# Group norm of a pair's outputs by two whole-tile sums, with its squares on ScalarE

## The chip, the cores and the metric

The kernel runs on one core of one Trainium2 chip. The metric is the device time of one execution, in microseconds. The engines are PE (matrix products), DVE (vector work), ACT (activations and copies), POOL and SP; SP and ACT also issue DMAs. Each engine works through a queue of its own, and semaphores join them.

## The reference

One layer of a decoder trunk, 512 positions of width 2048, in float32. Half of the width is an RWKV-7 group of 16 heads of 64 channels. Its recurrence gives for each position and head a vector `y` of 64 outputs, which is then normalized over the 64 channels of its head:

```python
def head_group_norm(y, w, b):
    B, T, H, N = y.shape
    mean = jnp.mean(y, axis=-1, keepdims=True)
    var = jnp.mean(jnp.square(y - mean), axis=-1, keepdims=True)
    yn = (y - mean) * lax.rsqrt(var + GN_EPS)
    return yn.reshape(B, T, H * N) * w.astype(jnp.float32) + b.astype(jnp.float32)
```

A bonus term is added, the sum is multiplied by a gate, joined with the pooled half, projected by `w_out` and added to the input; a gated embedding and an RMS norm follow.

## The kernel before

The input is normalized and transposed once into 16 tiles of channels by positions, each split in two parts, `hhi` and `hlo`; every large product is three matmuls on such parts (`mm3`, L164). The projections are computed in units of 128 output columns, 48 matmuls of 128x512 each. A generator (`stream`, L461) yields them one after another, and `pump(n)` (L492) takes about `n` matmuls from it.

The RWKV group goes in 8 pairs of heads, j = 0 to 7. `recur(j, ...)` (L753) runs the recurrence of a pair over 8 chunks of 64 positions. It is a chain of small matmuls, DVE and ACT steps, with `pump` calls between them, so that PE works on projections while the chain moves. DVE meanwhile solves the triangular systems of the next pair (`invert`, L650). At the end of chunks 3 and 7 ACT copies four heads-by-chunk blocks of `py` into `ysb` (L827), a tile of 128 positions by 4 x 2 x 64 channels: 8 groups of 64 channels in each partition.

Then comes the group norm that the change rewrites (L838 to L852). `y8` is `ysb` seen as 8 groups. Each group gets a `bn_stats` and a `bn_aggr` on DVE, for mean and variance; 64e-5 is added; `rsqrt` (L142) makes the reciprocal root of the 8 variances in eleven steps on 128x8 numbers, an estimate from the bits and three Newton rounds (L143 to L151); and each group is scaled by a `tensor_scalar` with its own mean and factor (L851). `finish` (L854) is put on a list.

Next, `gather(j + 1)` (L678) starts the following pair: `decay_and_rate` (L517; its DVE steps are L526, L533 and the scan L534), transposes of `v` and `bk`, `pump(H4)`, `norm_key` (L563, its DVE step L568), `pump(H5)`, and only then the pending `finish` of pair j: PE transposes `ysb` into `pyt` (L858), ACT scales it into `yo` (L860), DVE adds the bonus and multiplies by the gate (L861, L862), and ACT's queue stores it. Behind that, DVE transposes `x1` (L723) for the small products `pq`, `pmv` and `px`, and `scale_key` takes a reciprocal of 128x512 (L572) and a product (L573). `prepare(j + 1)` (L577) has the DVE steps L591 to L601. Weights come in chunks through four buffers; each is rounded on ACT (L132) and its rest taken on DVE (L133).

The framework places each engine's instructions itself, by readiness and priority, so that steps of different functions interleave in a queue. PE's matmuls of this stage are pinned to program order (`pin`, L154). `issue_after` holds a step behind another, and `high_priority` draws the recurrence's steps forward.

Of the kernel before, what the change touches and what calls it, by code (L numbers as in the profile page):

```python
# [9 lines left out]
F32 = mybir.dt.float32  # L10
F32R = mybir.dt.float32r
I32 = mybir.dt.int32
AF = mybir.ActivationFunctionType
ALU = mybir.AluOpType

P = 128
# [7 lines left out]
C = 64  # L24
# [10 lines left out]
def trunk_kernel(ctx: ExitStack, tc: tile.TileContext, x, p, norm_g, w_in, mu, w0, w_up, a0, a_up,  # L35
                 k_k, k_a, r_k, ln_w, ln_b, w_pool, pool_scale, w_out, w_ple, w_pg, b_pg, final_g, out):
    nc = tc.nc
# [104 lines left out]
    def rsqrt(y, v, t):  # L142
        nc.vector.tensor_scalar(y.bitcast(I32), v.bitcast(I32), -0.5, float(0x5F3759DF), ALU.mult, ALU.add)  # L143
        nc.vector.tensor_scalar(v, v, -0.5, None, ALU.mult)
        for _ in range(3):
            if v.shape[-1] * v.shape[1] == 1:
                nc.vector.scalar_tensor_tensor(t, y, v, y, ALU.mult, ALU.mult)
            else:
                nc.vector.tensor_tensor(t, y, v, ALU.mult)
                nc.vector.tensor_tensor(t, t, y, ALU.mult)  # L150
            nc.vector.scalar_tensor_tensor(y, t, 1.5, y, ALU.add, ALU.mult)  # L151
# [55 lines left out]
    for kind, nm, j in jobs:  # L207
# [7 lines left out]
        else:  # L215
            g, i = j // 4, j % 2
# [124 lines left out]
    rw = s2a.enter_context(tc.tile_pool(name="rw", bufs=1))  # L341
# [411 lines left out]
    def recur(j, work, between):  # L753
        d = st_.pop(j)
        pw, ar, mt, bv, uv, bkn, mv, x1 = (d[n_] for n_ in ("pw", "ar", "mt", "bv", "uv", "bkn", "mv", "x1"))
# [79 lines left out]
            pass  # L835


        st = rw.tile([P, 8, 6], F32, name=f"st{j}", tag="st")  # L838
        mvr = rw.tile([P, 8, 2], F32, name=f"mvr{j}", tag="mvr")
        y8 = ysb.rearrange("p q (h c) -> p (q h) c", h=2)  # L840
        for i in range(8):
            nc.vector.bn_stats(st[:, i, :], y8[:, i, :])
        for i in range(8):
            nc.vector.bn_aggr(mvr[:, i, :], st[:, i, :])
        rs8 = rw.tile([P, 8, 1], F32, name=f"rs8{j}", tag="rs8")
        ve8 = rw.tile([P, 8, 1], F32, name=f"ve8{j}", tag="ve8")
        nc.vector.tensor_scalar(ve8, mvr[:, :, 1:2], 64e-5, None, ALU.add)
        nt8 = rw.tile([P, 8, 1], F32, name=f"nt8{j}", tag="nt8")
        rsqrt(rs8, ve8, nt8)
        for i in range(8):  # L850
            nc.vector.tensor_scalar(y8[:, i, :], y8[:, i, :], mvr[:, i, 0:1], rs8[:, i, :],  # L851
                                    ALU.subtract, ALU.mult)  # L852

        def finish():  # L854
            sg = need("g", j)
# [29 lines left out]
    for j in range(NJ):  # L885
        def between():
            pump(H3 if j + 1 < NJ else HC[2])
            if j + 1 < NJ:
                scores(j + 1)
                pump_to(H2)  # L890

        if j + 1 == NJ:
            pn.append(rw.tile([P, NT, DPLE], F32, name="pn", tag="ar", bufs=2))
            for h in range(2):
                nc.scalar.dma_start(out=pn[0][:, 2 * h:2 * h + 2, :],
                                    in_=p[256 * h:256 * h + 256, :].rearrange("(t p) q -> p t q", p=P))
        if j + 1 < NJ:
            prepare(j + 1)
        recur(j, invert(j + 1) if j + 1 < NJ else iter(()), between)
        if j + 1 < NJ:  # L900
            gather(j + 1)
# [276 lines left out]
```

## Time and profile before

| | |
|---|---|
| time, median of 3 runs | 1094.54 us (1093.39 to 1097.44) |
| time of the profiled execution | 1094.06 us |
| its span, first to last instruction | 1092.3 us |
| PE, DVE, ACT busy | 1067.4, 707.9, 448.2 us |
| mean granted clock of PE | 0.998 |

Rows of a timeline give start and length in microseconds, the engine, the line, the operation, the tile written and those read, and the shapes; in brackets stands the idle time ahead of the row and what ended it. "x4" merges four neighbours. A busy PE is not PE at its peak: matmuls of 128x512 overlap, so that each has a recorded length of about 0.39 us while they start about 0.23 us apart.

### The profile page before, as it was taken

To read this page: it belongs to the slowest core of one execution; us is meant where nothing else is said; L and a number is where in the kernel's file an instruction comes from. 1 tells how busy PE (TensorE), PEld (TensorE's weight loads), DVE (VectorE), ACT (ScalarE), POOL (GpSimd) and SP (SyncE) were. 2 spreads that over 40 slices of the span, in tenths; PEclk is the share of its full clock that TensorE was granted. 3 is DMA by queue.
4 is the path that set the end of the run, shared out by engine and by line. 5 is a ranking of instruction groups with operands and counts; after the bars stand their busy time and mean duration, and the time that the engine had idled before them with its cause. 6 is when DMAs were issued, how large, how long until landed. Compare 5 with 4: busy or idle time off the path is not lost.

```text
span 1092.3 us, 17194 instructions
## 1 busy us (share of the span) xinstructions
PE 1067.4 (98%) x6060; PEld 879.1 (80%) x6060; DVE 707.9 (65%) x1835; ACT 448.2 (41%) x917; POOL 74.4 (7%) x180
## 2 busy tenths in 40 slices
PE   5999999999999999999999999999999999999996
PEld 4888878888888888787888788888888888888885
DVE  6687867878779679678886956454433424445366
ACT  7633534435335335353443344544222222233337
POOL 2100010110110110100101101000000000000000
PEclk9999999999999999999999999999999999999999
DMA  7433433332423333333334242774534438454534
GB/s 233 116 97 97 112 92 79 102 101 72 127 81 102 105 91 89 95 83 90 94 93 120 79 138 94 231 242 163 171 123 141 164 97 261 129 187 147 174 105 154
DMA packets 178485, 138.56 MB, mean 127 GB/s; under 512 B 34677, under 2 KB 139742, under 8 KB 178398
## 3 DMA queue, kind: packets, MB, share of 16 engines
q1 hardware_dynamic: 157694, 103.89, 32.2%
q10 hardware_dynamic: 20704, 33.56, 9.5%
q8 instruction: 48, 0.79, 0.3%
q14 instruction: 39, 0.32, 0.1%
HBM read 118.02 MB, written 18.87 MB: 125 GB/s over the span
## 4 chain that ended last, share of the span: by engine, by line
PE 88%; DVE 5%; DMA 3%; ACT 2%; issue 1%; SPq 0%; ACTq 0%; DVEq 0%
PE acc_o L157 16%; PE acc_g L157 16%; PE zb L157 15%; PE zv L157 8%; PE zr L157 7%; PE zg L157 7%; PE zk L157 6%; DMA n<-nd 2%; PE py L157 2%; PE pple L157 2%; PE pu L157 2%; PE pm L157 1%; PE pp L157 1%; PE ps L157 1%; PE pmv L157 1%
## 5 line engine op out<-in xcount | busy, mean ns | idle before, releaser
L133 DVE TENSOR_TENSOR wlo_g<-raw_g,whi_g 128x512 fp32r<-128x512 f32 x84 | 56.9, 683 | 78.7 <-ACT whi_g L132 78.5
L157 PE MATMUL zb<-hhi,whi_b 128*128 128x512 f32 x256 | 106.3, 415 | 0.0
L133 DVE TENSOR_TENSOR wlo_o<-raw_o,whi_o 128x512 fp32r<-128x512 f32 x64 | 43.9, 690 | 92.3 <-ACT whi_o L132 92.2
L157 PE MATMUL zb<-hhi,wlo_b 128*128 128x512 f32 x256 | 100.5, 393 | 0.0
L157 PE MATMUL acc_o<-whi_o,ylo 128*128 128x512 f32 x256 | 100.2, 391 | 0.0
L157 PE MATMUL acc_o<-whi_o,yhi 128*128 128x512 f32 x256 | 99.9, 390 | 0.0
L157 PE MATMUL zb<-hlo,whi_b 128*128 128x512 f32 x256 | 99.8, 390 | 0.0
L157 PE MATMUL acc_o<-wlo_o,yhi 128*128 128x512 f32 x256 | 99.7, 389 | 0.0
L132 ACT CAST whi_g<-raw_g 128x512 fp32r<-128x512 f32 x84 | 51.9, 620 | 105.5 <-PE acc_g L157 60.3
L157 PE MATMUL acc_g<-whi_g,x2hi 128*128 128x512 f32 x208 | 81.2, 391 | 0.0
L157 PE MATMUL acc_g<-wlo_g,x2hi 128*128 128x512 f32 x208 | 81.0, 389 | 0.0
L157 PE MATMUL acc_g<-whi_g,x2lo 128*128 128x512 f32 x208 | 80.6, 389 | 0.0
L132 ACT CAST whi_o<-raw_o 128x512 fp32r<-128x512 f32 x64 | 39.9, 623 | 97.8 <-PE acc_o L157 97.8
L813 POOL TENSOR_SCALAR s0p<-sbd,pw 64x64 f32<-64x64 f32 x96 | 56.7, 590 | 338.5 <-DVE sbd L806 253.7
L132 ACT CAST whi_b<-raw_b 128x512 fp32r<-128x512 f32 x64 | 39.7, 620 | 87.1 <-PE zv L157 34.9
L133 DVE TENSOR_TENSOR wlo_b<-raw_b,whi_b 128x512 fp32r<-128x512 f32 x64 | 43.7, 684 | 34.2 <-ACT whi_b L132 33.0
L157 PEld LDWEIGHTS zb<-hhi,wlo_b 128*128 128x128 f32 x256 | 48.0, 188 | 11.0
L661 DVE TENSOR_TENSOR xw<-xw,tm 128x60 f32<-128x60 f32 (+24 forms) x248 | 51.9, 209 | 6.8
L157 PEld LDWEIGHTS acc_o<-wlo_o,yhi 128*128 128x128 f32 x256 | 48.1, 188 | 10.0
L157 PEld LDWEIGHTS acc_o<-whi_o,ylo 128*128 128x128 f32 x256 | 48.1, 188 | 9.9
L157 PEld LDWEIGHTS acc_o<-whi_o,yhi 128*128 128x128 f32 x256 | 48.1, 188 | 9.6
L157 PEld LDWEIGHTS zb<-hhi,whi_b 128*128 128x128 f32 x256 | 48.3, 189 | 8.4
(285 smaller groups left out, 2546.8 us busy)
## 6 DMA issues: line engine op xcount, KB each, us to landing
raw_b<-in_w_in_dram SPq DMA_DIRECT2D x64, 256.0 KB
raw_o<-in_w_out_dram SPq DMA_DIRECT2D x64, 256.0 KB
raw_g<-in_w_pg_dram SPq DMA_DIRECT2D x64, 256.0 KB
raw_k<-in_w_in_dram SPq DMA_DIRECT2D x32, 256.0 KB
raw_r<-in_w_in_dram SPq DMA_DIRECT2D x32, 256.0 KB
raw_v<-in_w_in_dram SPq DMA_DIRECT2D x32, 256.0 KB
raw_g<-in_w_in_dram SPq DMA_DIRECT2D x32, 256.0 KB
n<-nd SPq DMA_DIRECT2D x16, 256.0 KB
```

The costliest lines, as they stand in the source:

```text
L132: nc.scalar.copy(hi, raw)
L133: nc.vector.tensor_tensor(lo, raw, hi.bitcast(F32), ALU.subtract)
L157: i = nc.tensor.matmul(*a, **k)
L661: nc.vector.tensor_tensor(xw[:, 0:n_, s + 1:32], xw[:, 0:n_, s + 1:32], tm[:, 0:n_, 0:w_], ALU.add)
L813: nc.gpsimd.tensor_scalar(s0p[hc, :], nxt[hc, hc], pcn[hc], None, ALU.mult)
```

## The change

The statistics of the 8 groups are taken over the whole tile. A sum over the channels (L840) is multiplied by -1/64 (L841) and added to `y8` as a broadcast operand (L842); ACT squares the centred tile into `ysq`, which takes the place of the tile `mv` (L844); a second sum (L846), scaled and raised by 64e-5 (L848), goes to `rsqrt`; and one product with the broadcast factors (L851) scales the tile. The functions behind it are the same, and from here on their lines have numbers lower by one.

```diff
-        st = rw.tile([P, 8, 6], F32, name=f"st{j}", tag="st")
-        mvr = rw.tile([P, 8, 2], F32, name=f"mvr{j}", tag="mvr")
         y8 = ysb.rearrange("p q (h c) -> p (q h) c", h=2)
-        for i in range(8):
-            nc.vector.bn_stats(st[:, i, :], y8[:, i, :])
-        for i in range(8):
-            nc.vector.bn_aggr(mvr[:, i, :], st[:, i, :])
+        mn8 = rw.tile([P, 8, 1], F32, name=f"mn8{j}", tag="mn8")
+        nc.vector.tensor_reduce(mn8, y8, mybir.AxisListType.X, ALU.add)
+        nc.vector.tensor_scalar(mn8, mn8, -1.0 / C, None, ALU.mult)
+        nc.vector.tensor_tensor(y8, y8, mn8.to_broadcast([P, 8, C]), ALU.add)
+        ysq = rw.tile([P, 8, C], F32, name=f"ysq{j}", tag="mv")
+        nc.scalar.activation(ysq, y8, AF.Square)
+        ve8 = rw.tile([P, 8, 1], F32, name=f"ve8{j}", tag="ve8")
+        nc.vector.tensor_reduce(ve8, ysq, mybir.AxisListType.X, ALU.add)
         rs8 = rw.tile([P, 8, 1], F32, name=f"rs8{j}", tag="rs8")
-        ve8 = rw.tile([P, 8, 1], F32, name=f"ve8{j}", tag="ve8")
-        nc.vector.tensor_scalar(ve8, mvr[:, :, 1:2], 64e-5, None, ALU.add)
+        nc.vector.tensor_scalar(ve8, ve8, 1.0 / C, 64e-5, ALU.mult, ALU.add)
         nt8 = rw.tile([P, 8, 1], F32, name=f"nt8{j}", tag="nt8")
         rsqrt(rs8, ve8, nt8)
-        for i in range(8):
-            nc.vector.tensor_scalar(y8[:, i, :], y8[:, i, :], mvr[:, i, 0:1], rs8[:, i, :],
-                                    ALU.subtract, ALU.mult)
+        nc.vector.tensor_tensor(y8, y8, rs8.to_broadcast([P, 8, C]), ALU.mult)
```

The order of PE's matmuls is the same in both programs. On DVE and ACT it is not. A row below names the line, the operation, the tile written, the tiles read and the shape; the number behind a tile's name counts tiles. This is DVE in the kernel before, from the second Newton round of pair 0's `rsqrt` (`rs`, `nt`) to the reciprocal of the next pair's key norm (`kk`):

```order
L149 TENSOR_TENSOR nt_2347<-rs_2344,ve_2345 128x8
L526 TENSOR_TENSOR us_2598<-ur_2595,us_2598 64x128
L150 TENSOR_TENSOR nt_2347<-nt_2347,rs_2344 128x8
L151 SCALAR_TENSOR_TENSOR rs_2344<-nt_2347,rs_2344 128x8
L149 TENSOR_TENSOR nt_2347<-rs_2344,ve_2345 128x8
L533 TENSOR_SCALAR sig_2382<-sig_2382 128x512
L150 TENSOR_TENSOR nt_2347<-nt_2347,rs_2344 128x8
L534 SCALAR_TENSOR_TENSOR sig_2382<-seg,sig_2382 128x512
L151 SCALAR_TENSOR_TENSOR rs_2344<-nt_2347,rs_2344 128x8
L591 TENSOR_SCALAR kp_2605<-tha_2394,dprm 128x512
L851 TENSOR_SCALAR ysb_1663<-ysb_1663,mvr_2327,rs_2344 128x64 x5
```

In the changed program the same stretch of DVE ends with these rows, the last of them the product that completes pair 0's `ysb`:

```order
L723 STREAM_TRANSPOSE y_2489<-x_2258 32x256
L133 TENSOR_TENSOR wlo_b_3_1403<-raw_b_3_1400,whi_b_3_1402 128x512
L151 SCALAR_TENSOR_TENSOR rs_2334<-nt_2336,rs_2334 128x8
L370 SCALAR_TENSOR_TENSOR sv_2430<-zv_2227,prm,sv_2430 128x511
L149 TENSOR_TENSOR nt_2336<-rs_2334,ve_2332 128x8
L572 RECIPROCAL kk_2349<-kk_2349 128x512
L150 TENSOR_TENSOR nt_2336<-nt_2336,rs_2334 128x8
L596 TENSOR_TENSOR bk_2586<-kp_2587,ipw_2369 128x4x2x64
L151 SCALAR_TENSOR_TENSOR rs_2334<-nt_2336,rs_2334 128x8
L573 SCALAR_TENSOR_TENSOR kk_2349<-sk_2076,prm,kk_2349 128x512
L851 TENSOR_TENSOR ysb_1663<-ysb_1663,rs_2334 128x512
```

Before, the scalings of `ysb` stand ahead of L568, L723, L572 and all behind them. Now the transposes, the reciprocal and steps of `prepare` stand between the Newton steps, ahead of L851.

The second place is the beginning of the same work in pair 2, on DVE; `st` and `mvr` are the statistics, `us`, `sig`, `kp` and `ar` belong to pair 3. Before:

```order
L842 BN_STATS st_4253<-ysb_3576 128x6 x4
L844 BN_AGGR mvr_4254<-st_4253 128x2 x4
L847 TENSOR_SCALAR ve_4272<-mvr_4254 128x8
L143 TENSOR_SCALAR rs_4271<-ve_4272 128x8
L144 TENSOR_SCALAR ve_4272<-ve_4272 128x8
L149 TENSOR_TENSOR nt_4274<-rs_4271,ve_4272 128x8
```

And in the changed program:

```order
L840 TENSOR_REDUCE mn_4217<-ysb_3540 128x8
L841 TENSOR_SCALAR mn_4217<-mn_4217 128x8
L842 TENSOR_TENSOR ysb_3540<-ysb_3540,mn_4217 128x512
L526 TENSOR_TENSOR us_4492<-ur_4489,us_4492 64x128
L533 TENSOR_SCALAR sig_4255<-sig_4255 128x512
L534 SCALAR_TENSOR_TENSOR sig_4255<-seg,sig_4255 128x512
L846 TENSOR_REDUCE ve_4223<-ysq_4221 128x8
L591 TENSOR_SCALAR kp_4499<-tha_4267,dprm 128x512
L848 TENSOR_SCALAR ve_4223<-ve_4223 128x8
L594 TENSOR_TENSOR ar_4497<-sr_4040,pw_4259 128x4x2x64
```

Here the scan L534 of the next pair has moved ahead of the second sum. The four early statistics, which before ran in the loop behind chunk 3, are gone from there.

The third place is ACT behind the last copies of `py` into `ysb`, pair 0. Before:

```order
L827 COPY ysb_1663<-py_4_2023 64x256 x2
L524 CAST us_2598<-ur_2595 128x128
L532 ACTIVATE sig_2382<-pu_2379,dprm 128x512
L547 ACTIVATE tha_2394<-pa_2391,dprm 128x512
L690 COPY uv_2396<-pv_2397 64x4x128
```

And now:

```order
L827 COPY ysb_1663<-py_4_2023 64x256 x2
L844 ACTIVATE ysq_2330<-ysb_1663 128x512
L532 ACTIVATE sig_2364<-pu_2361,dprm 128x512
L547 ACTIVATE tha_2376<-pa_2373,dprm 128x512
L690 COPY uv_2378<-pv_2379 64x4x128
```

The Square stands ahead of the next pair's `sig`, and waits there for the subtraction; the cast L524 has moved behind the copies of `bkn`.

## The prediction

> **What bounds the kernel now.** I read the page first, then the list of waits of PE, then the timelines of PE, DVE and ACT around the first group norm, and last the windows at both ends of the span, for the clock.
>
> ```profile
> PE 1067.4 (98%) x6060; PEld 879.1 (80%) x6060; DVE 707.9 (65%) x1835; ACT 448.2 (41%) x917; POOL 74.4 (7%) x180
> ...
> PE py L157 <- DVE sbd L806: 1.9, 6, 0.6
> PE pu L157 <- ACT x L745: 1.0, 1, 1.0
> PE pu L157 <- DVE zs L784: 0.7, 2, 0.4
> ```
>
> PE is the bound: it is busy for 98% of the span, and behind the first 30 us it waits for only 1.9 + 1.0 + 0.7 = 3.6 us. DVE is free a third of the time. So work taken off DVE is worth almost nothing, and what DVE delivers late to PE costs its full length. PE's order is pinned; whatever it waits for holds every matmul behind it. The one delivery of the group norm to PE is `ysb`, which `finish` transposes into `pyt`. Here is DVE at the end of pair 0, and the transposes:
>
> ```profile
> 182.69 0.61 DVE L842 BATCH_NORM_STATS2 st<-ysb 128x6 f32<-128x64 f32 x4 [0.32 <-ACT ysb L827]
> 183.21 0.36 DVE L844 BATCH_NORM_AGGREGATE mvr<-st 128x2 f32<-128x6 f32 x4
> 183.61 0.17 DVE L847 TENSOR_SCALAR ve<-mvr 128x8 f32<-128x8 f32 x1
> 183.81 0.17 DVE L143 TENSOR_SCALAR rs<-ve 128x8 int32<-128x8 int32 x1
> ...
> 185.83 0.42 DVE L533 TENSOR_SCALAR sig<-sig 128x512 f32<-128x512 f32 x1
> 186.16 0.16 DVE L150 TENSOR_TENSOR nt<-nt,rs 128x8 f32<-128x8 f32 x1
> 186.28 1.22 DVE L534 TENSOR_TENSOR_SCAN sig<-seg,sig 128x512 f32<-128x512 f32 x1
> 187.43 0.14 DVE L151 SCALAR_TENSOR_TENSOR rs<-nt,rs 128x8 f32<-128x8 f32 x1
> 187.49 0.54 DVE L591 TENSOR_SCALAR kp<-tha,dprm 128x512 f32<-128x512 f32 x1
> 187.94 1.20 DVE L851 TENSOR_SCALAR ysb<-ysb,mvr,rs 128x64 f32<-128x64 f32 x5
> 189.06 0.68 DVE L133 TENSOR_TENSOR wlo_b<-raw_b,whi_b 128x512 fp32r<-128x512 f32 x1
> 189.66 0.75 DVE L851 TENSOR_SCALAR ysb<-ysb,mvr,rs 128x64 f32<-128x64 f32 x3
> 190.33 0.68 DVE L568 TENSOR_SCALAR kk<-pss 128x512 f32<-128x512 f32 x1
> 190.93 0.89 DVE L723 STREAM_TRANSPOSE y<-x 32x256 f32<-32x256 f32 x2
> 191.86 3.35 DVE L572 RECIPROCAL kk<-kk 128x512 f32<-128x512 f32 x1
> ...
> 191.43 0.60 PE L161 MATMUL pyt<-ident,ysb 128*128 128x128 f32 x4
> ```
>
> `ysb` is normalized at 189.66 + 0.75 = 190.41, and PE reaches `pyt` at 191.43: a margin of 1.0 us. From the first statistic (182.69) to PE's need there are 8.7 us. That deadline, not the length of the group norm, is what the change must meet.
>
> **The change part by part.** DVE works through its queue in order. Start to start, an operation of 512 elements holds it a little less than its recorded length, since neighbours overlap: 0.60 for 0.68 (189.06 to 189.66), 0.33 for L533, 1.15 for the scan, 0.45 for L591, 3.27 for the reciprocal's 3.35. A 128x8 step between two long ones costs 0.06 to 0.12; I take 0.08.
>
> *The arithmetic alone* gets shorter. Per pair, 8 statistics, 8 aggregations and 8 scalings (1.20 + 0.75 + 2 x 0.61 + 2 x 0.36 = 3.9 us) give way to two sums, an addition, a multiplication and a 128x8 step. No row shows a reduction of this size; its bounds are the one-input L533 (0.42) and the two-input L133 (0.68); I take 0.68, since L568, with one input too, takes as long. The broadcast operations have two inputs: 0.68. That is about 2.9 us. The Square on ACT is put between the two rows below, of 0.69 and 0.64, and a handoff to ACT costs 0.1 (`pw` starts at 187.60, the scan before it ends at 187.50): about 0.8 us in which this chain waits.
>
> ```profile
> 184.71 0.69 ACT L532 ACTIVATE sig<-pu,dprm 128x512 f32<-128x512 f32 x1
> ...
> 187.60 0.64 ACT L539 ACTIVATE pw<-sig 128x512 f32<-128x512 f32 x1 [0.57 <-DVE rs L151]
> ```
>
> *The order* is what changes most. A sum over the whole tile cannot start before the last `ysb` copy, so the four early statistics of the loop go, and the variance waits for ACT. Meanwhile `sig`, `tha` and `pw` of the next pair arrive, and the built program places one long operation of the next pair's preparation behind nearly every small step of `rsqrt`. In an in-order queue each is paid in full, the reciprocal among them. Pair 0: L840 starts at 182.69, the subtraction ends at 184.3, Square at 185.0, L846 starts at 185.1 and holds 0.60. Then come L533 0.33, scan 1.15, L591 0.45, L592 0.60, L593 0.33, two weight splits 1.20, L594 0.60, L568 0.60, the two transposes 0.80, L370 0.66, reciprocal 3.27, L596 0.60, L573 0.66, together 11.25; twelve small steps, 1.0; and L851, 0.68. The end is 185.1 + 0.6 + 11.25 + 1.0 + 0.7 = 198.6, where PE wants `ysb` at 191.43: **PE waits 7.2 us**.
>
> ```profile
> L573 DVE SCALAR_TENSOR_TENSOR kk<-sk,prm,kk 128x512 f32<-128x512 f32 x8 | 6.2, 777 | 0.0
> ...
> 256.64 0.61 DVE L842 BATCH_NORM_STATS2 st<-ysb 128x6 f32<-128x64 f32 x4 [1.01 <-ACT ysb L827]
> 265.63 0.27 PE L161 MATMUL pyt<-ident,ysb 128*128 128x128 f32 x1
> 332.12 0.60 DVE L842 BATCH_NORM_STATS2 st<-ysb 128x6 f32<-128x64 f32 x4
> 340.50 0.27 PE L161 MATMUL pyt<-ident,ysb 128*128 128x128 f32 x1
> 407.27 0.60 DVE L842 BATCH_NORM_STATS2 st<-ysb 128x6 f32<-128x64 f32 x4 [1.01 <-ACT ysb L827]
> 416.01 0.38 PE L161 MATMUL pyt<-ident,ysb 128*128 128x128 f32 x2
> 481.12 0.60 DVE L842 BATCH_NORM_STATS2 st<-ysb 128x6 f32<-128x64 f32 x4 [0.32 <-ACT ysb L827]
> 489.87 0.38 PE L161 MATMUL pyt<-ident,ysb 128*128 128x128 f32 x2
> 555.95 0.61 DVE L842 BATCH_NORM_STATS2 st<-ysb 128x6 f32<-128x64 f32 x4 [1.01 <-ACT ysb L827]
> 566.41 0.27 PE L161 MATMUL pyt<-ident,ysb 128*128 128x128 f32 x1
> ...
> 638.03 0.44 DVE L723 STREAM_TRANSPOSE y<-x 32x256 f32<-32x256 f32 x1 [0.96 <-DMA x<-xd]
> 641.24 0.38 PE L161 MATMUL pyt<-ident,ysb 128*128 128x128 f32 x2
> ```
>
> The other pairs have the same sum with other fillers; L573 and its like (L370, L597, L601, L437) hold DVE 0.66, two-input ones 0.60, a 256-wide weight split half of that. Pair 1 has one split in Square's shadow and the 256-wide one for the other: 15.9 - 1.2 + 0.3 = 15.0 us, against 265.63 - 256.64 = 9.0: 6.0. In pair 2 Square stands behind `sig` on ACT, and L533 and the scan ahead of the squared sum, which ends at 5.0 instead of 3.0; behind it 10.8 of fillers, with L597, L599 and L601 among them, 1.0 and 0.7: 17.4, against 8.4: 9.0. Pair 3 has a split less, L597 for L370: 15.2 against 8.7: 6.5. Pair 4 has two pool additions for L370 and L596: 15.9 against 8.75: 7.2. Pair 5 has the pool gate's operations for a split, L370 and L573: 15.5 against 10.5: 5.1. Pair 6 has no such preparation, but the transpose L723, which waits for a DMA until 638.03, now stands ahead of the squared sum. From 638.5 there follow the sum 0.6, a split 0.3, twelve small steps, 0.2 apart like L847 and L143 above since each needs the last, the other transpose 0.4 and L851: 642.9 with 641.24 wanted, 1.7. Pair 7 keeps its margin. Sum: 7.2 + 6.0 + 9.0 + 6.5 + 7.2 + 5.1 + 1.7 = **42.7 us**.
>
> *What hides nothing, what is late next.* Everything behind `pyt` on PE starts that much later, and nothing fills PE meanwhile. DVE, having done the next pair's preparation, then runs ahead, so the later waits shrink: 1.5 of the 3.6 us, chosen as the 1.0 for `x1` and half of the 0.7 for `zs` and a little of `sbd`. On ACT, the store of `yo` moves ahead of the `q2` copies and waits for L861, some 4 us behind L851, just when PE reaches `pq`: 0 to 0.8 us a pair, which I leave in the range.
>
> *The clock.* A PE that stands still loses speed:
>
> ```profile
> 1083.34 0.28 PE L157 MATMUL acc_h<-whik,x2lo 128*128 128x256 f32 x1
> 1086.00:1090.00 4.00, 0.00 (x0) 0.00 (x0) 1.44 (x4) 1.57 (x4) 0.00 (x0) 0.81 0.56 207
> 1090.00:1092.30 2.30, 0.00 (x0) 0.00 (x0) 0.00 (x0) 0.00 (x0) 0.00 (x0) 0.50 0.29 96
> 12.51 1.54 PE L285 MATMUL pt_h<-ident,xt 128*128 128x128 f32 x6 [1.83 <-DVE xt L269]
> 16.91 0.38 PE L285 MATMUL pt_h<-ident,xt 128*128 128x128 f32 x2
> ```
>
> The last matmul ends at 1083.6. A mean of 0.81 over four microseconds means half clock from 1088.5: 4.9 us of idleness. At the other end six transposes take 1.54 us, 0.21 apart; at 16.91, 4.4 us later, they stand 0.11 apart. So a wait beyond 4.9 us should be followed by up to 4.4, say 4.2 us at half speed, 2.1 us lost. Six waits are longer than 4.9, one barely, so I count five: **10.5 us**. The Trainium skill, "TensorE: Matmul & The Clock Gate", Part 1, states that the clock halves after one idle window of about 3.4 us and that the windows run freely; by that rule a wait of 5 or 6 us may escape. The tail's 4.9 us agrees with it.
>
> The sum, against the profiled execution's own 1094.06 us (span 1092.3 and 1.8 around it, 0.5 under the median): 1094.1 + 42.7 + 10.5 - 1.5 = **1146 us**, +4.7%.
>
> **The rivals.** *Full clock.* The waits come, but the clock isn't taken away, since a wait falls between two windows or is shorter than summed: 1094.1 + 42.7 - 1.5 = 1135. For it: the waits of 5 to 7 us are near the one observed 4.9. Against it: four of them are clearly longer.
>
> *A longer half clock.* Each wait costs 3.4 us of lost work instead of 2.1, all six count, and ACT's `q2` comes late (6 x 0.8 = 5): 1094.1 + 42.7 + 20.4 + 5 - 1.5 = 1161. For it: the slow stretch at the start is seen once only.
>
> *Not slower.* DVE does 3.9 - 2.9 = 1.0 us less a pair, and the part that used to sit in the loop is gone from there; if the scaling still reaches PE in time, only PE's waits for DVE and ACT can shrink, 3.6 us at most: 1090.5. The point from which it decides is 8.7 us from L840 to the end of L851 in pair 0, and it needs the long fillers to weigh 4 us instead of 11. The rows of those fillers speak against it. The Trainium skill, "VectorE: DVE Perf Modes", "Rules for kernel authors", says to minimize the operation count, by which this change gains; the trace agrees that eight scalings take longer (1.95) than one operation (0.68), but that work has no weight against the deadline.
>
> **How the numbers follow.** Forecast 0.55; full clock 0.27; longer half clock 0.10; not slower 0.04; the remaining 0.04 lies between 1095 and 1125. The unknown prices move the sum little: a reduction at 0.42 gives 2 x 0.26 x 6 = 3 us back, one at twice 0.68 costs 8. The range runs from 1126 (full clock, the cheap reductions and another 6 us of fillers hidden) to 1159, and leaves out the top of the third case and all below. A measurement of this kernel can tell 0.5%, 5.5 us, from no change. Faster by more than that cannot come from 3.6 us of waits: 0.02. Same: 0.03. Slower: 0.95.
>
> **What would show it.** In the changed profile, PE's list of waits should gain `pyt` <- DVE `ysb`, six times, 5 to 9 us each, about 41 us together; in DVE's timeline the reciprocal should stand ahead of L851 in pairs 0 to 5; the windows behind each `pyt` should show a granted clock under 1. If `pyt` waits under 2 us in these pairs, the sum over the queue is wrong; if it waits as summed and the clock stays 1.00, only the clock term is.

## The result and the profile after

| | before | after |
|---|---|---|
| median of 5 runs | 1094.67 us (1093.39 to 1097.44) | 1148.49 us (1147.75 to 1149.96) |
| ratio to before | | 1.0489, interval 1.0472 to 1.0507 |
| span of the profiled execution | 1092.3 us | 1147.5 us |
| mean granted clock of PE | 0.998 | 0.978 |

The changed kernel is slower by 4.9%, 2.5 us over the forecast of 1146 and inside its range. The profiled execution took 1149.29 us. The busy line of the page, PE's row of the 40 slices with the granted clock under it, and PE's list of waits (total, times, longest; in us) say where the time went.

```profile
PE 1081.2 (94%) x6060; PEld 888.9 (77%) x6060; DVE 702.3 (61%) x1683; ACT 452.4 (39%) x925; POOL 69.7 (6%) x180
...
PE   5999997997997997997998999999999999999996
...
PEclk9999999998998998998999999999999999999998
...
```

```profile
PE pyt L161 <- DVE ysb L851: 34.3, 6, 8.6
PE pyt L161 <- DVE sw L420: 7.3, 1, 7.3
...
PE py L157 <- DVE sbd L806: 3.6, 6, 1.5
...
```

DVE did what was meant: 152 instructions fewer and 5.6 us less work (707.9 to 702.3). PE does the same matmuls, but dips six times, in every third slice; one slice is 28.7 us, and a pair takes about three. The second row of the waits is the same wait in pair 4: L420 stands directly behind L851 in DVE's queue, and the list took its end for the release.

This is DVE at pair 0's norm (start, length, engine, line, operation, tiles, and the idle time ahead); the rows left out between the second sum and the last steps are of the same kind as those shown behind them.

```profile
182.31 0.69 DVE L840 TENSOR_REDUCE mn<-ysb 128x8 f32<-128x512 f32 x1 [0.32 <-ACT ysb L827]
...
183.24 0.69 DVE L842 TENSOR_TENSOR ysb<-ysb,mn 128x512 f32<-128x512 f32 x1
184.69 0.69 DVE L846 TENSOR_REDUCE ve<-ysq 128x8 f32<-128x512 f32 x1 [0.76 <-ACT ysq L844]
...
193.01 0.15 DVE L149 TENSOR_TENSOR nt<-rs,ve 128x8 f32<-128x8 f32 x1
193.09 3.34 DVE L572 RECIPROCAL kk<-kk 128x512 f32<-128x512 f32 x1
196.35 0.10 DVE L150 TENSOR_TENSOR nt<-nt,rs 128x8 f32<-128x8 f32 x1
196.37 0.67 DVE L596 TENSOR_TENSOR bk<-kp,ipw 128x512 f32<-128x512 f32 x1
196.96 0.15 DVE L151 SCALAR_TENSOR_TENSOR rs<-nt,rs 128x8 f32<-128x8 f32 x1
197.04 0.74 DVE L573 SCALAR_TENSOR_TENSOR kk<-sk,prm,kk 128x512 f32<-128x512 f32 x1
197.70 0.68 DVE L851 TENSOR_TENSOR ysb<-ysb,rs 128x512 f32<-128x512 f32 x1
```

Between 193.01 and 197.04 the norm advances by three steps of 0.1 to 0.15 us; the rest of these four microseconds is the next pair's work. DVE is never idle here, and nothing in it is slow. It simply does the less urgent work first. On PE, the last product of `zb` ahead of the wait, and the transposes behind it:

```profile
190.95 0.39 PE L157 MATMUL zb<-hhi,wlo_b 128*128 128x512 f32 x1
198.53 1.09 PE L161 MATMUL pyt<-ident,ysb 128*128 128x128 f32 x4 [7.18 <-DVE ysb L851]
```

Three stretches of this place, the wait and what follows (bounds, length, then busy time of PE, PEld, DVE, ACT and POOL with the number of instructions, then the granted clock, the DMA share and GB/s):

```profile
...
191.10:198.50 7.40, 0.24 (x2) 0.00 (x1) 7.34 (x14) 0.98 (x2) 0.00 (x0) 0.81 0.21 60
198.50:202.50 4.00, 3.97 (x12) 3.32 (x13) 4.00 (x7) 1.90 (x3) 0.00 (x0) 0.50 0.00 0
202.50:212.00 9.50, 9.50 (x131) 7.87 (x129) 2.78 (x6) 3.85 (x10) 0.40 (x1) 1.00 0.34 99
```

The middle row is the second price: for the 4 us behind the wait PE is as busy as ever, at half clock.

The waits below count from where PE could have gone on: 0.23 us behind the start of the last long matmul, as the neighbours stand apart, not from the end of its record. So pair 0 counts 198.53 - (190.95 + 0.23) = 7.34 (7.35 in these rounded rows) where the bracket says 7.18. Over the pairs 0 to 7 that gives 7.3, 6.5, 8.8, 6.8, 7.4, 5.4, 0.5 and 0.2, together 42.8 us. The six stretches of half clock that reach past a wait go on by 4.0, 6.0, 4.0, 5.5, 3.7 and 2.9 us; half of their 26.1 us is lost, 13.1. The two make 55.9, and the spans differ by 55.2.

### The profile page after: what moved, and what is told of

Same layout as the page of the kernel before. It is cut to its first block, busy times and chain, and to the rows that moved or that the text cites. A ratio compares the mean times of both kernels' runs of the same rounds, so it can differ in the third digit from the quotient of the medians.

```text
span 1147.5 us, 17061 instructions
## 1 busy us (share of the span) xinstructions
PE 1081.2 (94%) x6060; PEld 888.9 (77%) x6060; DVE 702.3 (61%) x1683; ACT 452.4 (39%) x925; POOL 69.7 (6%) x180
## 4 chain that ended last, share of the span: by engine, by line
PE 82%; DVE 10%; ACT 2%; issue 2%; DMA 2%; SPq 0%; ACTq 0%; DVEq 0%
PE acc_o L157 15%; PE acc_g L157 15%; PE zb L157 12%; PE zv L157 7%; PE zk L157 7%; PE zr L157 7%; PE zg L157 6%; PE py L157 2%; DVE kk L572 2%; PE pple L157 1%; PE pu L157 1%; DMA n<-nd 1%; PE pm L157 1%; PE ps L157 1%; PE pp L157 1%
## 5 line engine op out<-in xcount | busy, mean ns | idle before, releaser
L157 PE MATMUL zb<-hhi,whi_b 128*128 128x512 f32 x256 | 109.7, 428 | 0.0
L157 PE MATMUL zb<-hhi,wlo_b 128*128 128x512 f32 x256 | 102.8, 402 | 0.0
L157 PE MATMUL zb<-hlo,whi_b 128*128 128x512 f32 x256 | 102.4, 400 | 0.0
L813 POOL TENSOR_SCALAR s0p<-sbd,pw 64x64 f32<-64x64 f32 x96 | 53.0, 553 | 343.3 <-DVE sbd L806 263.2
L157 PEld LDWEIGHTS zb<-hlo,whi_b 128*128 128x128 f32 x256 | 50.2, 196 | 8.6
```

The source lines that it names most:

```text
L157: i = nc.tensor.matmul(*a, **k)
L813: nc.gpsimd.tensor_scalar(s0p[hc, :], nxt[hc, hc], pcn[hc], None, ALU.mult)
```

## The experiments

Theory: DVE's queue is the cause. The two sums and the trip to ACT open gaps in the norm's chain, the order puts the next pair's long steps into them, and PE, whose order is fixed, waits for the end of that queue and then runs at half clock for a while. Rivals: the new operations themselves are slow (the reductions, the broadcasts, the trip to ACT); or the waits alone are the cost, and the clock is a trait of the records.

**The order alone.** The changed kernel, with the next pair's preparation issued behind the product:

```diff
+    def behind_norm():
+        return tc.issue_after(done[0].ins) if done[0] is not None else ExitStack()
...
-        late[0] = nc.vector.tensor_scalar(kk, ps, 1e-24, None, ALU.max)
+        with behind_norm():
+            late[0] = nc.vector.tensor_scalar(kk, ps, 1e-24, None, ALU.max)
```

Likewise for L591, L593 and L594; `done[0]` is the product L851. Every operation of the change is kept.

> The changed kernel with the same arithmetic, but with the DVE steps of the next pair's preparation (the maximum of the key norm, and with it the transposes of x1 and the reciprocal; the first steps of prepare) held behind the product that completes ysb. Queue theory (the wait of PE comes from what stands ahead of that product in DVE's queue): pair 0's product ends near 191.1 us against 191.4 wanted, PE waits at pyt for at most 1 us a pair, the clock stays full: 1094 to 1100. Rival, length theory (the sums over the whole tile, the trip to ACT and the chain of small steps are themselves too long for PE's deadline): it stays above 1130.

Measured: 1097.95 us (1097.26 to 1100.13), ratio 1.0037 (1.0023 to 1.0050). Here the numbers of the lines behind L515 are higher by 3 to 6. DVE around pair 0's product in this kernel:

```profile
188.75 0.69 DVE L133 TENSOR_TENSOR wlo_b<-raw_b,whi_b 128x512 fp32r<-128x512 f32 x1
189.36 0.16 DVE L150 TENSOR_TENSOR nt<-nt,rs 128x8 f32<-128x8 f32 x1
...
190.16 0.17 DVE L151 SCALAR_TENSOR_TENSOR rs<-nt,rs 128x8 f32<-128x8 f32 x1
190.36 0.69 DVE L857 TENSOR_TENSOR ysb<-ysb,rs 128x512 f32<-128x512 f32 x1
...
193.75 3.35 DVE L576 RECIPROCAL kk<-kk 128x512 f32<-128x512 f32 x1
```

```profile
...
PE pm L157 <- DVE bk L606: 1.3, 2, 0.9
...
PE pyt L161 <- DVE ysb L857: 0.9, 2, 0.6
```

The product ends at 191.05 instead of 198.38, in time for PE, and the waits at `pyt` come to 0.9 us in this list (1.4 over all pairs, counted as above). 50.5 of the 53.8 us are back with the same operations on the same engines, so the operations' own length cannot hold more than the rest. The next pair's preparation, now later, takes something back: PE's product `pm` waits for `bk`.

**One filler.** Only `scale_key` (the reciprocal L572 and L573) is put behind the product:

```diff
-            with tc.issue_after(yt.ins):
+            with tc.issue_after((done[0] or yt).ins):
                 scale_key(j + 1)
```

> The changed kernel with only scale_key (the reciprocal, 3.27 us, and the product behind it) held behind the product that completes ysb; the built program moves some shorter steps of prepare up in their place. Queue theory: the fillers shrink by 2.6, 2.6, 4.3, 3.1, 2.7 and 2.6 us in pairs 0 to 5, which leaves waits of about 4.7, 3.9, 4.5, 3.7, 4.7 and 2.8, 24 us together, most of them too short for the clock to halve (3 us lost): about 1121. Length theory: unchanged, 1148.

Measured: 1127.01 us in one run. The waits in pairs 0 to 5 are 4.8, 4.0, 4.7, 4.0, 4.8 and 2.8:

```profile
PE pyt L161 <- DVE ysb L851: 19.9, 6, 4.7
...
PE pyt L161 <- DVE sw L420: 4.7, 1, 4.7
```

Each wait is within 0.3 us of what was expected. In pair 0 the wait is 2.5 us shorter than in the changed kernel, and DVE's rows show how that comes about:

```profile
...
193.67 0.75 DVE L597 SCALAR_TENSOR_TENSOR ar<-sk,dprm,pw 128x512 f32<-128x512 f32 x1
...
194.41 0.74 DVE L601 SCALAR_TENSOR_TENSOR kp<-sr,dprm,kp 128x512 f32<-128x512 f32 x1
195.07 0.68 DVE L851 TENSOR_TENSOR ysb<-ysb,rs 128x512 f32<-128x512 f32 x1
195.68 3.35 DVE L572 RECIPROCAL kk<-kk 128x512 f32<-128x512 f32 x1
```

The reciprocal (3.27) and L573 (0.66) went out of the chain, and the gaps were filled with L597 and L601 (0.66 each): 2.6 us less. The order fills a gap with whatever is ready. The time is 6 us over what was expected, for a reason of its own: waits of 4 us still lost the clock, in five places and by 9.3 us, where 3 was expected.

**The deadline instead of the queue.** If PE's wait is the end of the queue less PE's need, then a later need must cover it, with DVE's order left alone. `finish` is taken from the list at the end of `gather` in place of behind `pump(H5)`, first in the changed kernel and, as a control, in the kernel before:

```diff
-        if pending:
-            pending.pop()()
         pump(HX)
...
         pump(2 * H1)
+        if pending:
+            pending.pop()()
```

> The changed kernel, in which the pending finish of pair j (the transposes into pyt and what follows) is no longer issued behind pump(H5) but at the end of gather(j + 1), behind pump(2 * H1). The product L851 keeps its place in DVE's queue, behind the next pair's preparation; only PE's deadline is moved, by some 9 us of matmuls. Theory (PE waits exactly as long as its deadline lies ahead of the end of DVE's queue): the waits at pyt were 7.3, 6.5, 8.8, 6.8, 7.4, 5.4 us, so all are covered, pair 2 nearly; no wait of 1 us is left at pyt, the clock is not halved in the middle of the span, and the time is 1094 to 1099 us. Rival (it is the amount of the preparation in the stage, or its own delay to pq, pmv and px, that PE pays for; the wait only moves to another place): the waits at pq, px or py grow by what goes at pyt, and the time stays above 1130.

> The kernel before with the same later place of finish, as a control. Theory: its waits at pyt were nil, so a later deadline has nothing to cover; 1092 to 1097 us, the same as before within 0.3%. Rival (the later place saves PE something of its own, so that the run beside it owes its time to that): faster than 1090.

Measured: the changed kernel with the later place takes 1093.35 us (1092.01 to 1095.24), ratio 0.9982 (0.9974 to 0.9991); the control 1095.03 (1092.77 to 1097.38), ratio 0.9990 (0.9980 to 1.0000). Two rows of DVE in the first of them, PE's transposes, then the stretch in which the changed kernel waits, then the one long row of its waits behind the start:

```profile
193.07 3.35 DVE L572 RECIPROCAL kk<-kk 128x512 f32<-128x512 f32 x1
...
198.49 0.68 DVE L851 TENSOR_TENSOR ysb<-ysb,rs 128x512 f32<-128x512 f32 x1
```

```profile
199.84 0.60 PE L161 MATMUL pyt<-ident,ysb 128*128 128x128 f32 x4
```

```profile
191.10:198.50 7.40, 7.40 (x119) 6.09 (x119) 7.34 (x13) 4.30 (x10) 0.77 (x1) 1.00 0.24 69
...
```

```profile
PE py L157 <- DVE sbd L806: 3.4, 6, 1.5
...
```

The reciprocal still stands ahead of L851, and the product ends at 199.17, later than in the changed kernel. But PE comes to `pyt` only at 199.84, and no wait for `ysb` is left in the list. The rival, by which the waits move to `pq`, `px` or `py`, is refuted: `pq` and `px` do not appear, and `py` waits for 3.4 us where it waited for 3.6 in the changed kernel. So the queue is harmless as long as it ends before PE needs it. This version stands 0.2% below the kernel before, which took 1096.07 us beside it: too little to call it faster. The control, 0.1% below, is too close to it to say how much of that is the place of `finish` alone.

**Which edit opens the gaps.** Three kernels with a part of the change: the squares on DVE (no trip to ACT); the statistics of before with two whole-tile broadcast operations for the scaling; and the statistics over the whole tile (the two sums with the subtraction and the squares) with the scaling group by group.

```diff
-        nc.scalar.activation(ysq, y8, AF.Square)
+        nc.vector.tensor_tensor(ysq, y8, y8, ALU.mult)
```

> The changed kernel with the squares taken on DVE, so that the chain makes no trip to ACT. The long steps of the next pair still stand between the Newton steps in the built program. Queue theory: the 0.8 us of waiting gives way to 0.6 us of work, and the fillers decide: 1143 to 1153. Length theory with the trip to ACT as its cause: below 1125.

```diff
+        nc.vector.tensor_tensor(y8, y8, mvr[:, :, 0:1].to_broadcast([P, 8, C]), ALU.subtract)
+        nc.vector.tensor_tensor(y8, y8, rs8.to_broadcast([P, 8, C]), ALU.mult)
```

> The kernel before with its own statistics of eight groups, early ones included, and only the scaling by two whole-tile operations with broadcast operands. Queue theory: the chain starts as before, the built program interleaves a little more, waits sum to about 2 us: 1094 to 1099. If broadcast operands were what costs the time: above 1120.

```diff
-        nc.vector.tensor_tensor(y8, y8, rs8.to_broadcast([P, 8, C]), ALU.mult)
+        for i in range(8):
+            nc.vector.tensor_scalar(y8[:, i, :], y8[:, i, :], rs8[:, i, :], None, ALU.mult)
```

> The changed kernel with its two sums, but the scaling group by group (eight operations) as before. Queue theory: the sums are what moves the chain behind the next pair's preparation, the form of the scaling is not; PE can start on the first groups 0.2 us earlier a pair: 1144 to 1150. If the whole-tile product were the cause: below 1125.

| | us | ratio | waits at `pyt`, us |
|---|---|---|---|
| squares on DVE | 1145.59 (one run) | | 41.6 |
| scaling only | 1095.44 | 1.0012 (1.0002 to 1.0022) | 1.8 |
| sums only | 1148.82 (one run) | | 40.7 |

The statistics over the whole tile carry the loss, whether or not ACT takes the squares; the trip to ACT is worth about 3 us by one run, whose waits are 1.2 us shorter. Which step of these statistics matters most was not separated. The broadcast scaling is harmless.

**The clock.** The changed kernel, with 24 needless products of 128x512 ahead of `pyt` in pairs 0 to 5: PE does not get to `pyt` earlier, but stands still for less.

```diff
+            for _ in range(24 if j < 6 else 0):
+                mm(ps, blk, hhi[:, 0, :], start=True, stop=True)
```

> The changed kernel with 24 needless products of 128x512 (0.227 us each, 5.45 us) in front of the transposes of ysb in pairs 0 to 5; they write the bank that the transposes then overwrite, so the result is the same. They lie in PE's wait and shorten its idle part to about 1.9, 1.0, 3.3, 1.3, 2.0 and 0 us. If the halved clock is a cost of its own: it stays full in at least five of the six places, and about 13 us less the little that pair 5 may lose come back: 1135 to 1139, although PE has 144 products more. If the clock term is not real, and the whole loss is the wait: 1148 or more.

Measured: 1137.01 us (1135.09 to 1138.66), ratio 1.0395 (1.0380 to 1.0411). Pair 0 on PE and the stretch around it:

```profile
191.57 5.60 PE L157 MATMUL pyt<-hhi,blk 128*128 128x512 f32 x24
...
198.85 0.66 PE L161 MATMUL pyt<-ident,ysb 128*128 128x128 f32 x4 [1.68 <-DVE ysb L851]
```

```profile
188.00:206.00 18.00, 16.32 (x159) 13.25 (x158) 16.33 (x34) 8.29 (x20) 0.40 (x1) 1.00 0.21 62
```

With PE kept at work the clock stays 1.00, and the kernel is 11.5 us faster with 144 more matmuls in it. That is the clock's share of the loss, measured by itself, against 13.1 from the stretches. It is known to some 3 us only: against the kernel before measured beside each, the loss goes from 53.8 to 43.2 us, 10.6 less, while the profiled execution alone, 1135.09, is 13.4 under the changed kernel's median. The other three runs show a mean clock of 0.995 or 0.996 where the profiled one shows 0.998, so some clock was lost there again. One wait in the profiled execution is 3.2 us long (pair 2), and it too left the clock at 1.00.

**Waits of chosen length.** The held kernel of the first experiment, with needless reciprocals ahead of the product in every pair: one of 128x256, then two of 128x512.

```diff
+        scr = rw.tile([P, 8, C], F32, name=f"scr{j}", tag="mv")
+        nc.vector.reciprocal(scr[:, 0:4, :], y8[:, 0:4, :])
         done[0] = nc.vector.tensor_tensor(y8, y8, rs8.to_broadcast([P, 8, C]), ALU.mult)
```

> The kernel of the first experiment (next pair's preparation held back), with one needless reciprocal of 128x256 a pair (half of 3.3 us) put ahead of the product that completes ysb; nothing reads it. Queue theory: DVE's work ahead of that product reaches PE one for one past a margin of a few tenths: waits of 2.5, 1.9, 2.5, 1.5, 2.4, 1.0, 2.3 and 1.8 us, together 16, and little of the clock: 1111 to 1120. Rival: such a delay is taken up by the work that PE has queued and by earlier buffers: below 1102.

> As the run with the half reciprocal, with two whole ones (6.5 us) a pair. Queue theory with the clock: each wait grows by 4.9 us to 6 to 7.4, together 55, and each is followed by a half clock that costs about 2.2: 17 more, so 1094.7 + 3 + 55 + 17 = 1170 (1163 to 1176). Without a clock term: 1153.

Measured: 1118.28 us (1115.73 to 1120.13), ratio 1.0219 (1.0197 to 1.0241), with waits of 18.1 us in all; and 1164.4 in one run, with 57.4. Each dose reaches PE's wait at `pyt` in full: the waits are within 2.4 us of the sums expected. The times are not quite the sum. The long dose lost 15.6 us to the clock, where 17 was expected; with its waits that gives 1097.4 - 1.4 + 57.4 + 15.6 = 1169.0 from the held kernel's profiled execution, 4.6 us more than measured, and where these came back stays open. In the short dose the clock was the surprise: five of the eight waits, of 2.1 to 2.9 us, lost 8.4 us to it in the profiled execution. Three of these waits, in windows of 3.41 us; the first of each pair of rows holds the wait and the second is what follows:

```profile
425.21:428.63 3.42, 1.86 (x11) 1.35 (x10) 3.25 (x11) 0.72 (x2) 0.00 (x0) 1.00 0.22 57
428.63:432.04 3.41, 3.41 (x16) 2.53 (x14) 3.35 (x3) 1.89 (x4) 0.00 (x0) 1.00 0.21 63
268.20:271.61 3.41, 1.49 (x10) 1.01 (x9) 3.18 (x12) 0.64 (x3) 0.00 (x0) 1.00 0.38 106
271.62:275.03 3.41, 3.41 (x10) 2.64 (x9) 3.38 (x2) 0.96 (x2) 0.00 (x0) 0.50 0.03 10
...
503.72:507.13 3.41, 1.50 (x9) 1.35 (x10) 3.41 (x12) 0.78 (x1) 0.00 (x0) 1.00 0.28 79
507.13:510.54 3.41, 2.58 (x12) 1.78 (x10) 3.38 (x7) 1.25 (x2) 0.00 (x0) 1.00 0.06 14
```

PE idle for 3.42 - 1.86 = 1.56 us of a window: full clock behind it. Idle for 3.41 - 1.49 = 1.92: the next window at half. The third wait is the longest of the three, 2.85 us, but 0.93 us of it lie in the window before; it leaves 3.41 - 1.50 = 1.91 in this one, and costs no clock.

## Why the prediction was right

**The queue.** Right, nearly row by row. In pair 0 the first sum starts 0.38 us earlier than the first statistic did; PE is 0.25 us earlier there too, and the reason was not tested. L846 then starts 2.38 us behind L840 where 2.4 was summed, and from L846 to the end of L851 it is 13.69 where 13.5 was summed. The product ends at 198.38, forecast 198.6. The waits of the pairs were forecast as 7.2, 6.0, 9.0, 6.5, 7.2, 5.1, 1.7 and 0; they are 7.3, 6.5, 8.8, 6.8, 7.4, 5.4, 0.5 and 0.2. The sum of 42.8 for 42.7 owes something to luck, since pair 6 fell short by 1.2 and the others made up for it.

**The prices not in the trace of before.** These are the groups of the new operations (line, engine, tiles, shapes, count; busy time and mean ns of one; idle time ahead and its end):

```profile
L842 DVE TENSOR_TENSOR ysb<-ysb,mn 128x512 f32<-128x512 f32 x8 | 5.5, 691 | 0.3
L840 DVE TENSOR_REDUCE mn<-ysb 128x8 f32<-128x512 f32 x8 | 5.5, 685 | 3.7 <-ACT ysb L827 3.7
L846 DVE TENSOR_REDUCE ve<-ysq 128x8 f32<-128x512 f32 x8 | 5.4, 680 | 2.2 <-ACT ysq L844 2.2
L851 DVE TENSOR_TENSOR ysb<-ysb,rs 128x512 f32<-128x512 f32 x8 | 5.4, 676 | 0.1
L844 ACT ACTIVATE ysq<-ysb 128x512 f32<-128x512 f32 x8 | 5.0, 628 | 3.9 <-DVE ysb L842 3.5 <-DVE wlo_wp L133 0.5
```

The reduction takes 0.685 and 0.680 us, the 0.68 that was taken rather than the 0.42 of its lower bound; a broadcast operand costs nothing extra; the Square, at 0.63, is just under the rows it was put between (0.64 and 0.69).

**Pair 6.** The step that gave 1.7 kept the deadline of before, 641.24 - 638.03 = 3.2 us from the start of the first transpose to `pyt`. The chain was as long as summed, but PE came 4.55 us behind that start:

```profile
691.04 0.44 DVE L723 STREAM_TRANSPOSE y<-x 32x256 f32<-32x256 f32 x1 [1.15 <-DMA x<-xd]
...
695.32 0.69 DVE L851 TENSOR_TENSOR ysb<-ysb,rs 128x512 f32<-128x512 f32 x1
```

The product ends at 696.01 and PE waited 0.5 us. A start set by a DMA does not keep its distance to PE's program from one kernel to the other.

**What comes late next.** The store of `yo` on ACT, left in the range at 0 to 0.8 us a pair, has no wait of PE for `q2` to show, so 0 holds. The give-back of 1.5 is not there as described. The 1.0 for `x1` is gone, but the wait for `sbd` grew by 1.7 (1.9 to 3.6) where it was to shrink: together 0.7 more. With these the parts make 55.9 + 0.7 = 56.6 us, the spans differ by 55.2, and where the other 1.4 us came back stays open.

**The clock.** The mechanism was right, the size low: 13.1 us for 10.5. The profiled execution went 55.2 us up where the sum had 51.7, and this is 2.6 of those 3.5. The step that failed is "a wait beyond 4.9 us ... so I count five". All six waits lost the clock, the 5.4 of pair 5 too, and 2.2 us each on average (1.5 to 3.0) for the 2.1 assumed. That the average came so near owes something to luck, since the 2.1 was taken from one stretch at the start of the span and the six spread by a factor of two. The tail of the span, from which 4.9 us was taken, only told what idleness is enough, not what is needed. The rival with a full clock (1135) is refuted by the windows and by the filled waits: these came to 1137.0 with 42 us of waits and needless products, which is that rival's world made by hand. The rule of the Trainium skill, "TensorE: Matmul & The Clock Gate", Part 1, that one idle window of about 3.4 us halves the clock and that the windows run freely, agrees with these runs in the window's length (3.41 us) and in the free grid, but not in the whole idle window: 1.92 us of one was enough.

**Not slower.** The price of the fillers decided, as said: with them held the same operations end at 191.05, and the kernel is within 0.4% of before. What the Trainium skill, "VectorE: DVE Perf Modes", "Rules for kernel authors", says of minimizing the operation count did not help: DVE runs 152 operations fewer, and the kernel is slower.

## What to carry to other kernels

Shortening work on an engine that is not the bound earned nothing by itself here (5.6 us less of DVE's work, 53.8 us more time); what counted was when the last step of its chain left an in-order queue, against when the pinned engine asked for it. A chain of small dependent steps is a row of gaps for a scheduler to fill, so replacing eight early, independent pieces by one late whole-tile step can cost the length of everything that gets in between. Read the built order between the chain's first and last step, sum it, and compare it with the deadline; if it misses, hold the fillers or move the deadline, and reckon that each wait of PE above some 2 us may cost half-clock time too.

## What the runs showed of the hardware that was not expected

The granted clock is set for fixed windows of 3.413 us: in each trace all its changes lie on one grid of that step. What a window at full clock leads to goes by how long PE's records leave it idle there. Over the traces of the changed kernel and its variants (from 30 to 1060 us), those with up to 1.91 us idle were followed by full clock and those with 1.95 us or more by half; in between, one of 1.92 was followed by half and one of 1.94 by full. So some 56% of a window is enough. A wait of 3.2 us went free where the grid cut it in two (1.21 and 1.86 us, in the kernel with needless products), and one of 2.1 us cost a window at half clock, 1.7 us of PE's work.

A window that is itself at half clock needs much less idleness to be followed by another: all 36 of them with up to 0.67 us idle were followed by full clock, all 32 with 0.83 us or more by half. In pair 1 of the changed kernel the window from 281.02 us holds the last 0.83 us of the wait, and the clock stays at half for all of the next window, in which PE is never idle. So how far a wait reaches into its last window decides what it costs behind its end; in the changed kernel each wait brought one to three windows at half clock.
